# S5 output stage: an even, weighted walk of its list, 8 KB scratch rows, and scan states that reach their operand layout through DRAM

## The chip, the core and the metric

The kernel runs on one core of a Trainium2 chip. The metric is the device time of one execution in microseconds (us), lower is better. Before the change the median of three runs is 1825.99 us (1824.85 to 1827.47).

## What is computed

Two layers over a sequence of 256 frames with 2048 channels: a chunked gated linear attention (GLA), then an S5 state-space layer. Only the second matters here. Cut to its core:

```python
proj = u_in @ w_in                                   # (256, 2048) @ (2048, 8192)
u, z = jnp.split(proj, 2, axis=-1)                   # 4096 channels each, 256 groups of 16
bu = einsum('blgi,gpi->blgp', u, bb)                 # 64 complex states for each group
x = scan over the frames: x[l] = lb * x[l-1] + bu[l]
y = Re(einsum('blgp,gip->blgi', x, c)) + d_skip * u
y = gelu(y)
y = y * sigmoid(y @ w_glu + b_glu) * silu(z)
h = y @ w_out
```

All of it is float32. The large products are made of three products of split operands (a high part and a remainder, `hi` and `lo`).

## The kernel before: its stages and what sets the order

The recurrence is taken in blocks of 8 frames, so a scan runs over 32 blocks (chunks) instead of 256 frames. What a block needs from the state at its start is one product, and what its frames give each other is another, with a Toeplitz operand. The 256 groups are taken 8 at a time, in 32 units `f`.

The stages of the S5 layer, in order of time:

- `su`: the u half of the input projection, in 8 groups of banks. Beside it the block operands are made (`b_pow`, `b_tr`, `s_mm`, `k_out`): the block inputs of the scan go into `sx`, the Toeplitz rows into the DRAM scratch `dk` (512 rows, pitch 1920 floats). A DRAM scratch `rec` (128 rows, 32 units of 384 floats) was filled in the GLA layer with the small tables of each unit.
- `sz`: the z half of the projection, again 8 groups `g` of 8 steps `kp`. A step splits a 512 KB weight tile (`hisz`, cast on ScalarE at L145; `losz`, subtraction on VectorE at L146) and issues 24 matmuls of 128x256. The split tiles have three buffers each, the weight tiles four. A group writes four banks of PSUM, and the pool `mm` has five. So the first quarter of a group's first step finds a free bank, and the second quarter waits until ScalarE has emptied the first bank of the group before (`zs`, SiLU, L1280). Steps are named here by group and step: step 2.0 works with `hisz20`, its banks are `sz20` to `sz23`.
- the S5 output stage: it lies in the shade of the `sz` groups 1 to 7, which are 56 steps. A list of small pieces is walked while the steps go by. In its order it has, for `f` from 0 to 33: up to three of the 30 scan steps of the second half (`scan`, L1183 to L1185), `cside(f)` (loads `cl` for unit f+1 and the Toeplitz tile `mt` for unit f, makes the two 128x1024 operands `wc`), `xstage(f-1)` and `ystage(f-2)`. `pump(Y_RATE)` pops 2.311 pieces at each step, whatever their size.
- `gl`: the GLU product with 4096x4096 weights, which reads the activated outputs `U`.

`xstage(f)` brings the chunk states into the layout of a matmul operand: VectorE turns 32x32 blocks of `sx` (L1237, tile `xT`), TensorE turns two 128x128 tiles of it (L1240, tile `psxs`), ScalarE copies them out of PSUM (L1242, tile `xS`). `ystage(f)` is 24 matmuls of 128x128 with 32 output partitions each: 8 with `mt` (L1252) and 16 with `wc` (L1255), four of them side by side on the array; the hardware has each as two. VectorE then turns the sum (L1258, `yt`), and ScalarE applies the GELU and writes it over `U` (L1259). GELU and SiLU are in different function tables, so a change between L1259 and L1280 loads a table.

`cload` fetches `cl` with three DMAs (L1213 once, L1215 twice, for rows in swapped halves), `mload` fetches `mt` with one DMA of 512 KB (L1229): 16 rows of `dk`, each read eight times, shifted by 512 B. `mt` and `wc` have two buffers, so the load of `mt` for unit f waits for the matmuls of unit f-2.

The order on each engine isn't that of the source. A scheduler of the tile layer places every instruction on its engine, by its own estimate of when its inputs are there; each engine then works strictly in its own order and waits where something isn't there. A DMA that SP or ScalarE issues takes one of eight completion semaphores (`DMAHW0` to `DMAHW7`), which the two queues share, and waits until the transfer that used this semaphore before has landed.

Of the kernel before, what the change touches and what calls it, by code (L numbers as in the profile page):

```python
# [33 lines left out]
def trunk(ctx, tc, x, c, ln_g, ln_b, ada_w, ada_b, gla_w_in, gla_gate_w2, gla_gate_b, gla_norm_g,  # L34
# [393 lines left out]

    vt = cp.tile([P, 104], F32, name="vt")
    gnT, gbT, bgluT, lngT, lnbT = vt[:, 0:32], vt[:, 32:40], vt[:, 40:72], vt[:, 72:88], vt[:, 88:104]  # L430

    def vectors():
        vr = tp.tile([104, P], F32, tag="vr", name="vr", bufs=1)
        rows = [(gla_norm_g[0], 32), (gla_gate_b[0], 8), (s5_b_glu[0], 32), (ln_g[0], 16), (ln_b[0], 16)]
        r0 = 0
        for ap, n in rows:
            dma(vr[r0:r0 + n, :], ap.rearrange("(k p) -> k p", p=P))
            r0 += n
        ps = psx("psv")
        PE.transpose(ps[:, :104], vr, ident[:104, :104])  # L440
        S.copy(vt, ps[:, :104])

    ada0 = ada_now(0, 0, 0, 2)
# [4 lines left out]
    abT = cp.tile([P, 64], F32, name="abT")  # L448
    ps = psx("psv2")
# [21 lines left out]
    dT = cp.tile([16, 256], F32, name="dT")  # L471

    def prep_small():
        dr = rp.tile([P, 2, 16], F32, tag="row", name="dr", bufs=2)
        dma(dr, s5_d[0].rearrange("(h g i) -> g h i", h=2, i=16))
        ps = psx("psd")
        for h in range(2):
            PE.transpose(ps[:16, h * P:(h + 1) * P], dr[:, h, :], ident)
        S.copy(dT, ps[:16, 0:256])
# [121 lines left out]
    def prep_pow(t):  # L601
# [6 lines left out]
        for ri in range(2):  # L608
            for nb in range(2):
# [5 lines left out]
                S.activation(lc[:, :, ri, :, nb * 4:nb * 4 + 4].rearrange("p f g n -> p n f g"), pv, AF.Identity, scale=sgn if ri else 1.0)  # L615
        wdma(rec[:, 16 * t:16 * t + 16, 128:256], lc.rearrange("p f r g n -> p f (r g n)"))

    def to_rows(src, i_of, t, o, nm):
        got = {}

        def step(ib):
# [7 lines left out]
            if ib == 3:  # L629
                av = a.rearrange("p (f g) i -> p f (g i)", f=16)  # L630
                wdma(rec[:, 16 * t:16 * t + 16, o:o + 128], av)

        return [lambda ib=ib: step(ib) for ib in range(4)]

    def prep_b(t):
# [21 lines left out]

        return [load], [comp] + to_rows(lambda: got["b"], lambda s, i: s[:, :, i], t, 256, f"b{t}")

    def prep_c(t):  # L660
# [14 lines left out]

        return [load], [comp] + to_rows(lambda: got["c"], lambda s, i: s[:, i].rearrange("g r p -> g (r p)"), t, 0, f"c{t}")

# [13 lines left out]
    SCAN_RATE = 1.728  # L691
    Y_RATE = 2.311
    qt, kt = qk
# [359 lines left out]
    def bload(f2):  # L1053

        a = tp.tile([P, 2, 384], F32, tag="rb", name=f"rb{f2}", bufs=2)
        dma(a[:, :, 0:256], rec[:, 2 * f2:2 * f2 + 2, 128:384])
        for h in range(2):
            dma(a[64 * h:64 * h + 64, :, 256:384], rec[64 - 64 * h:128 - 64 * h, 2 * f2:2 * f2 + 2, 256:384])
        rb[f2] = a
# [3 lines left out]
    def kload(f2):  # L1063

        a = rc[f2] = tp.tile([P, 2, 144], F32, tag="rc", name=f"rc{f2}", bufs=2)
        dma(a, rec[:, 2 * f2:2 * f2 + 2, 0:144])

# [93 lines left out]
    for p in range(18):  # L1161
# [5 lines left out]
        if p >= 2:  # L1167
            bq.append(lambda p=p: k_out(p - 2))

    bload(0)  # L1170
    b_pace = [0.0]

# [38 lines left out]
    def cload(f):  # L1211
        a = tp.tile([P, 384], F32, tag="cl", name=f"cl{f}", bufs=2)
        dma(a[:, 0:256], rec[:, f, 0:256])  # L1213
        for h in range(2):
            dma(a[64 * h:64 * h + 64, 256:384], rec[64 - 64 * h:128 - 64 * h, f, 0:128])  # L1215
        cl[f] = a

    def cunit(f):
        a = cl[f]
        w = [tp.tile([P, 8, 8, 16], F32, tag=f"wc{i}", name=f"wc{i}{f}", bufs=2) for i in range(2)]  # L1220
        powmul(w[0], w[1], a[:, 0:128], a[:, 256:384], a[:, 128:256])
        wc[f] = w
# [3 lines left out]
    def mload(f):  # L1226
        m = tp.tile([P, 8, 8, 16], F32, tag="mt", name=f"mt{f}", bufs=2)
        src = bass.AP(tensor=kap.tensor, offset=kap.offset + f * 16 * 1920, ap=[[1920, 16], [128, 8], [1, 1024]])
        dma(m.rearrange("p t g i -> p (t g i)"), src)  # L1229
        mt[f] = m  # L1230

    xss = {}

    def xstage(f):
        xt_ = tp.tile([P, 2, 4, 32], F32, tag="xt", name=f"xT{f}", bufs=1)
        n = 2 * (f % 16)
        V.transpose(xt_, sx[:, f // 16, 0:32, :, n:n + 2].rearrange("p c r b -> p b r c"))  # L1237
        px = psx(f"psxs{f}")
        for b in range(2):
            PE.transpose(px[:, b * P:(b + 1) * P], xt_[:, b].rearrange("p r l -> p (r l)"), ident)  # L1240
        xs = tp.tile([P, 2, 128], F32, tag="xs", name=f"xS{f}", bufs=2)
        S.copy(xs, px[:, :T].rearrange("p (b r) -> p b r", b=2))  # L1242
        xss[f] = xs

    def ystage(f):
# [3 lines left out]
        for b in range(2):  # L1249
# [3 lines left out]
            for w in wc[f]:  # L1253
                for q in range(4):
                    PE.matmul(o[32 * q:32 * q + 32], lhsT=xs[:, b, 32 * q:32 * q + 32],  # L1255
                              rhs=w[:, 2 * q + b].rearrange("p n i -> p (n i)"), start=False, stop=(w is wc[f][-1]))
        yt = tp.tile([P, 8, 32], F32, tag="yt", name=f"yt{f}", bufs=2)
        V.transpose(yt, py[:, :T].rearrange("p (b t i) -> p t b i", b=2, t=8))  # L1258
        S.activation(U, yt, AF.Gelu_apprx_tanh)  # L1259

    def cside(f):
# [3 lines left out]
        cunit(f)  # L1265

    zs = []
# [32 lines left out]
    while bg:  # L1300
        pump()

# [149 lines left out]
```

## Time and profile before

| | |
|---|---|
| median of three runs | 1825.99 us |
| profiled execution, its own time | 1828.37 us |
| its span | 1826.6 us |
| TensorE busy in the span | 97% |
| VectorE busy | 77% |
| ScalarE busy | 49% |
| GpSimd busy | 5% |
| S5 output stage (sz groups 1 to 7) | 1050.8 to 1277.6 us, 226.8 us |

Times inside the profile are microseconds from the start of the span. PE is TensorE, PEld its weight loads, DVE VectorE, ACT ScalarE, POOL GpSimd, SP SyncE, which issues nearly all DMAs; a q behind an engine's name is its queue. Matmuls are pipelined, so their busy time is modelled, and the distance from one start to the next tells more than the length of one. A row of a group gives lines, engine, operation, tiles and shapes, the count, then busy time and the mean of one in ns, then idle time of the engine just ahead of them and what ended it. "DMA share" is the mean busy share of the core's 16 DMA engines.

### The profile page before, as it was taken

What the parts mean: (1) busy time and instruction counts of PE and PEld (TensorE: products, weight loads), DVE (VectorE), ACT (ScalarE), POOL (GpSimd) and SP (SyncE); (2) the same over time, 40 slices, a digit from 0 to 9 for tenths busy, and PEclk for the clock granted to TensorE, in tenths of its full rate; (3) what the DMA queues carried; (4) which work ended last, traced back from release to release, by engine and by line L of the source; (5) the groups of instructions that cost most, each with busy time, mean ns of one, the idle gap of its engine ahead of it and who ended that gap; (6) DMA issues with size and microseconds to landing.
All of it is one profiled execution on the core that took longest, in us unless ns stands there. A gap on an engine that the chain in (4) does not pass through costs nothing.

```text
span 1826.6 us, 33659 instructions
## 1 busy us (share of the span) xinstructions
PE 1780.4 (97%) x13491; PEld 1573.1 (86%) x13491; DVE 1411.3 (77%) x1880; ACT 898.9 (49%) x1266; POOL 86.3 (5%) x94
## 2 busy tenths in 40 slices
PE   7999999999999999999999999999999999999997
PEld 5776897899999888799999999989888888888885
DVE  4887757879999988687789789889577775557556
ACT  4433557556556333655555544546545444444332
POOL 0000000000000000002224300000000000000000
PEclk9999999999999999999999999999999999999998
DMA  9996975879889998587666577999788886668553
GB/s 344 387 358 229 296 249 163 277 265 324 288 285 323 331 364 290 175 254 212 193 199 191 171 223 211 242 241 239 227 283 267 275 275 200 189 200 316 195 183 92
DMA packets 246101, 457.86 MB, mean 251 GB/s; under 512 B 19828, under 2 KB 49198, under 8 KB 244662
## 3 DMA queue, kind: packets, MB, share of 16 engines
q1 hardware_dynamic: 239320, 436.02, 74.4%
q0 software_dynamic: 5856, 18.63, 3.1%
q8 instruction: 106, 1.74, 0.4%
q10 hardware_dynamic: 768, 1.05, 0.2%
q14 instruction: 51, 0.42, 0.1%
HBM read 437.01 MB, written 18.61 MB: 249 GB/s over the span
## 4 chain that ended last, share of the span: by engine, by line
PE 83%; DVE 6%; DMA 5%; ACT 3%; issue 3%; SPq 1%; POOL 0%; DVEq 0%; ACTq 0%; POOLq 0%
PE gl L192 13%; PE gl L193 7%; PE op L168 6%; PE op L169 6%; PE op L167 6%; PE v L168 3%; PE z L182 3%; PE z L181 3%; PE z L180 3%; PE v L169 3%; PE v L167 3%; PE sz L180 3%; PE sz L182 2%; PE su L180 2%; PE sz L181 2%
## 5 line engine op out<-in xcount | busy, mean ns | idle before, releaser
L146 DVE TENSOR_TENSOR logl<-wgl,higl 128x1024 fp32r<-128x1024 f32 x128 | 156.7, 1224 | 116.3 <-ACT higl L145 114.6
L145 ACT CAST higl<-wgl 128x1024 fp32r<-128x1024 f32 x128 | 134.3, 1050 | 172.2 <-PE gl L192 165.4
L192 PE MATMUL gl<-yp,higl 128*128 128x512 f32 x512 | 179.9, 396 | 0.1
L192 PE MATMUL gl<-yb,higl 128*128 128x512 f32 x512 | 179.6, 396 | 0.0
L145 ACT CAST hio<-wo 128x1024 fp32r<-128x1024 f32 x95 | 100.2, 1055 | 153.0 <-PE op L169 134.8
L146 DVE TENSOR_TENSOR loo<-wo,hio 128x1024 fp32r<-128x1024 f32 x95 | 116.7, 1230 | 66.4 <-ACT hio L145 64.5
L317 DVE SCALAR_TENSOR_TENSOR acc<-wa,cs,acc 128x512 f32<-128x512 f32 x217 | 163.0, 751 | 2.7
L180 PE MATMUL su<-u1h,hisu 128*128 128x256 f32 x512 | 151.4, 297 | 0.0
L180 PE MATMUL sz<-u1h,hisz 128*128 128x256 f32 x512 | 150.1, 293 | 1.2 <-ACT zs L1280 1.2
L180 PE MATMUL z<-u0h,hiz 128*128 128x256 f32 x512 | 148.7, 290 | 0.0
L182 PE MATMUL su<-u1h,losu 128*128 128x256 f32 x512 | 145.3, 284 | 0.4 <-DVE losu L146 0.4
L182 PE MATMUL sz<-u1h,losz 128*128 128x256 f32 x512 | 144.5, 283 | 1.1 <-DVE losz L146 1.1
L182 PE MATMUL z<-u0h,loz 128*128 128x256 f32 x512 | 144.9, 283 | 0.6 <-DVE loz L146 0.6
L181 PE MATMUL su<-u1l,hisu 128*128 128x256 f32 x512 | 145.1, 284 | 0.0
L181 PE MATMUL z<-u0l,hiz 128*128 128x256 f32 x512 | 144.7, 283 | 0.0
L181 PE MATMUL sz<-u1l,hisz 128*128 128x256 f32 x512 | 144.5, 282 | 0.0
L193 PE MATMUL gl<-yb,logl 128*128 128x256 f32 x512 | 143.0, 279 | 0.0
L193 PE MATMUL gl<-yp,logl 128*128 128x256 f32 x512 | 142.3, 280 | 0.0
L145 ACT CAST hisz<-wsz 128x1024 fp32r<-128x1024 f32 x64 | 67.0, 1050 | 108.4 <-PE sz L181 60.2
L192 PEld LDWEIGHTS gl<-yp,higl 128*128 128x128 f32 x512 | 95.9, 188 | 23.3 <-issue 0.8
L192 PEld LDWEIGHTS gl<-yb,higl 128*128 128x128 f32 x512 | 96.1, 188 | 23.0
L145 ACT CAST hiz<-wz 128x1024 fp32r<-128x1024 f32 x64 | 67.2, 1052 | 89.0 <-PE z L181 79.4
(322 smaller groups left out, 5001.1 us busy)
## 6 DMA issues: line engine op xcount, KB each, us to landing
wgl<-in_s_w_glu SPq DMA_DIRECT2D x128, 512.0 KB, 4.8
wa<-in_ada_w SPq DMA_DIRECT2D x116, 512.0 KB, 5.3
wv<-in_gla_w_in SPq DMA_DIRECT2D x64, 512.0 KB, 6.2
wz<-in_gla_w_in SPq DMA_DIRECT2D x64, 512.0 KB, 5.0
wsu<-in_s_w_in SPq DMA_DIRECT2D x64, 512.0 KB, 4.2
wsz<-in_s_w_in SPq DMA_DIRECT2D x64, 512.0 KB, 5.7
wo<-in_s_w_out SPq DMA_DIRECT2D x64, 512.0 KB, 4.5
a<-in_ada_w SPq DMA_DIRECT2D x31, 1024.0 KB, 10.8
```

The lines of the kernel that those rows point to most:

```text
L145: S.copy(hi, w)
L146: last_lo[0] = V.tensor_tensor(lo, w, hi.bitcast(F32), op=ALU.subtract).ins
L167: PE.matmul(banks[tt], lhsT=uh, rhs=hi[:, kk, :], start=(k == first), stop=False)
L168: PE.matmul(banks[tt], lhsT=uh, rhs=lo[:, kk, :], start=False, stop=False)
L169: last_mm[0] = PE.matmul(banks[tt], lhsT=ul, rhs=hi[:, kk, :], start=False, stop=(k == last)).ins
L180: PE.matmul(o, lhsT=wh, rhs=u.hi(k), start=(k == first), stop=False)
L181: PE.matmul(o, lhsT=wh, rhs=u.lo(k), start=False, stop=False)
L182: last_mm[0] = PE.matmul(o, lhsT=wl, rhs=u.hi(k), start=False, stop=(k == last)).ins
L192: PE.matmul(banks[f], lhsT=hi[:, kk, fs], rhs=u.both(k), start=(k == 0), stop=False)
L193: PE.matmul(banks[f][:, :T], lhsT=lo[:, kk, fs], rhs=u.hi(k), start=False, stop=(k == last))
L317: V.scalar_tensor_tensor(acc[0], w[:, kk, :], cs[:, k:k + 1], acc[0], op0=ALU.mult, op1=ALU.add)
```

## The change

Four edits go together.

1. **The list.** `bg` and `Y_RATE` give way to a list `yq` of pieces with weights: 1.0 for a scan step, 2.5 for `cside`, 0.5 for `xwrite`, 0.0 for `xread`, 2.0 for `ystage`. The weights add up to 190, and each of the 56 steps is owed 190/56 of them; a piece is issued as soon as its weight is covered. There are two scan steps for each unit instead of three.
2. **Scratch rows.** A unit of `rec` takes 512 floats instead of 384 (a row of `rec` is 64 KB instead of 48), and a row of `dk` 2048 instead of 1920 (8 KB). The extra place in `rec` holds the tables with swapped halves, written by four more DMAs in the GLA layer, so that `cl` comes in one DMA with pieces of 1.5 KB.
3. **Scan states through DRAM.** `xstage` gives way to `xwrite` and `xread`. `xwrite(f)` copies the states of unit f on ScalarE into a dense tile `xT` (L1244, three buffers) and writes it to the DRAM scratch `dx` by a DMA on ScalarE's queue (L1245, 128 rows of 1 KB). `xread(f)` reads it back in operand layout on GpSimd's queue (L1249, tile `xS`, three buffers, pieces of 256 B). The two transposes of TensorE, the one of VectorE and the copy out of PSUM are gone. The partitions of `cl`, `wc` and `xS` are in another order (chunk, then quarter) to fit.
4. **Room.** `vt`, `abT` and `dT` leave the constant pool (`dT` goes through a DRAM scratch and is loaded again), and `yt` has one buffer instead of two.

```diff
-    rec = dp.tile([P, 32, 384], F32, name="rec")
-    dk = dp.tile([512, 1920], F32, name="dk")
+    rec = dp.tile([P, 32, 512], F32, name="rec")
+    dk = dp.tile([512, 2048], F32, name="dk")
+    dx = dp.tile([32, P, 256], F32, name="dx")
...
+                if o == 128:
+                    for h in range(2):
+                        wdma(rec[64 * h:64 * h + 64, 16 * t:16 * t + 16, 0:128], av[64 - 64 * h:128 - 64 * h])
...
     def cload(f):
         a = tp.tile([P, 384], F32, tag="cl", name=f"cl{f}", bufs=2)
-        dma(a[:, 0:256], rec[:, f, 0:256])
-        for h in range(2):
-            dma(a[64 * h:64 * h + 64, 256:384], rec[64 - 64 * h:128 - 64 * h, f, 0:128])
+        dma(a, rec[:, f, 0:384].rearrange("(r l) x -> l r x", r=4))
...
-    def xstage(f):
-        xt_ = tp.tile([P, 2, 4, 32], F32, tag="xt", name=f"xT{f}", bufs=1)
+    def xwrite(f):
+        xt_ = tp.tile([P, 4, 2, 32], F32, tag="xt", name=f"xT{f}", bufs=3)
         n = 2 * (f % 16)
-        V.transpose(xt_, sx[:, f // 16, 0:32, :, n:n + 2].rearrange("p c r b -> p b r c"))
-        px = psx(f"psxs{f}")
-        for b in range(2):
-            PE.transpose(px[:, b * P:(b + 1) * P], xt_[:, b].rearrange("p r l -> p (r l)"), ident)
-        xs = tp.tile([P, 2, 128], F32, tag="xs", name=f"xS{f}", bufs=2)
-        S.copy(xs, px[:, :T].rearrange("p (b r) -> p b r", b=2))
-        xss[f] = xs
+        S.copy(xt_, sx[:, f // 16, 0:32, :, n:n + 2].rearrange("p c r b -> p r b c"))
+        S.dma_start(dx[f], xt_.rearrange("p r b c -> p (r b c)"))
+
+    def xread(f):
+        xs = xss[f] = tp.tile([P, 4, 2, 32], F32, tag="xs", name=f"xS{f}", bufs=3)
+        wdma(xs.rearrange("p q b c -> p q (b c)"), dx[f].rearrange("(q l) (r x) -> (l r) q x", q=4, r=4))
...
-            pump(SCAN_RATE if g == 0 else Y_RATE)
+            if g == 0:
+                pump(SCAN_RATE)
+            else:
+                owed += yrate
+                while yq and owed >= yq[0][0]:
+                    owed -= yq[0][0]
+                    yq.pop(0)[1]()
...
+            yq.append((0.5, lambda: xwrite(0)))
             for f in range(34):
-                for _ in range(3):
-                    if sc1:
-                        bg.append(sc1.pop(0))
+                yq.extend((1.0, sc1.pop(0)) for _ in range(2) if sc1)
                 if f < 32:
-                    bg.append(lambda f=f: cside(f))
-                if 1 <= f < 33:
-                    bg.append(lambda f=f: xstage(f - 1))
+                    yq.append((2.5, lambda f=f: cside(f)))
+                    if f < 31:
+                        yq.append((0.5, lambda f=f: xwrite(f + 1)))
+                    yq.append((0.0, lambda f=f: xread(f)))
                 if f >= 2:
-                    bg.append(lambda f=f: ystage(f - 2))
+                    yq.append((2.0, lambda f=f: ystage(f - 2)))
+            yrate = sum(w_ for w_, _ in yq) / 56
```

How the change stands on two engines is shown by the built programs. First ScalarE at the start of the stage, before: from the cast for step 1.3 on, the casts of the weights follow each other, with a copy of turned states (`xS`, unit number behind it) between.

```order
L145 CAST hisz13_11540<-wsz13_11538 128x1024
L145 CAST hisz14_11591<-wsz14_11589 128x1024
L145 CAST hisz15_11629<-wsz15_11627 128x1024
L145 CAST hisz16_11676<-wsz16_11674 128x1024
L1242 COPY xS0_11583<-psxs0_11580 128x256
L145 CAST hisz17_11742<-wsz17_11740 128x1024
L145 CAST hisz20_11794<-wsz20_11792 128x1024
L1242 COPY xS1_11672<-psxs1_11669 128x256
```

ScalarE at the same place after the change, with the semaphores that an instruction waits for (`DMAHW` ones are transfers):

```order
L145 CAST hisz13_11555<-wsz13_11553 128x1024 [waits DMAHW2_49,PE_49]
L1244 COPY xT0_11453<-sx_7551 128x256 [waits DMASW4_49,DMAHW7_49,DMASW3_49,Pool_49]
L1244 COPY xT1_11502<-sx_7551 128x256
L1245 DMA dx_205<-xT0_11453 128x256 [waits Activation_49]
L1245 DMA dx_205<-xT1_11502 128x256 [waits Activation_49]
L1244 COPY xT2_11583<-sx_7551 128x256
L145 CAST hisz14_11598<-wsz14_11596 128x1024 [waits DMAHW3_49,PE_49]
L1245 DMA dx_205<-xT2_11583 128x256 [waits DMAHW4_49,Activation_49]
L1244 COPY xT3_11634<-sx_7551 128x256 [waits DMAHW0_49]
L1244 COPY xT4_11743<-sx_7551 128x256 [waits DMAHW2_49]
L1245 DMA dx_205<-xT3_11634 128x256 [waits DMAHW6_49,Activation_49]
L1245 DMA dx_205<-xT4_11743 128x256 [waits DMAHW7_49,Activation_49]
```

The scheduler has moved the writes of the first 16 units, whose states are all there when the stage begins, ahead of their place in the list: all 16 copies and DMAs stand between the casts for steps 1.3 and 2.1, two to four copies between two casts. The writes of units 16 to 31 stand in the same way between the casts for steps 4.3 and 5.1. In each of these stretches a copy waits for the write three units earlier, because `xT` has three buffers. In the first, write 5 waits for the semaphore of the load `mt0`. The SiLU copies of group 1 (`zs` from `sz10` to `sz13`) stand behind the cast for step 2.1 and one GELU, in both programs.

The other place is TensorE at the end of the stage. Before, from the last matmuls of unit 30 on (`x4` is four of them):

```order
L1255 MATMUL psy30_14585<-wc030_14408,xS30_14518 32x128 x4
L1255 MATMUL psy30_14585<-wc130_14409,xS30_14518 32x128 x4
L180 MATMUL sz70_14218<-u1h1_7422,hisz76_14615 128x256
L181 MATMUL sz70_14218<-u1l1_7424,hisz76_14615 128x256
L182 MATMUL sz70_14218<-u1h1_7422,losz76_14616 128x256
```

Here unit 30 comes ahead of step 7.6, unit 31 ahead of step 7.7. After:

```order
L1261 MATMUL psy30_14528<-wc030_14365,xS30_14372 32x128 x4
L1261 MATMUL psy30_14528<-wc130_14366,xS30_14372 32x128 x4
L1258 MATMUL psy31_14560<-mt31_14462,U3_7557 32x128 x4
L1261 MATMUL psy31_14560<-wc031_14464,xS31_14468 32x128 x4
L1261 MATMUL psy31_14560<-wc131_14465,xS31_14468 32x128 x4
L1258 MATMUL psy31_14560<-mt31_14462,U3_7557 32x128 x4
L1261 MATMUL psy31_14560<-wc031_14464,xS31_14468 32x128 x4
L1261 MATMUL psy31_14560<-wc131_14465,xS31_14468 32x128 x4
L192 MATMUL gl00_14604<-yp0_14600,higl00_14610 128x512
```

Unit 29 now stands ahead of step 7.7, and units 30 and 31 follow each other behind it, ahead of the first matmul of the GLU product. In the middle of the stage a unit comes every second step up to unit 13 and two units every three steps from there on; before, they came at two in three to five steps while the scan steps lasted, and then mostly one at every step with a gap in each fourth or so.

More of the change, by code (lines that the diff above doesn't have):

```diff
@@ L441, in vectors @@
         S.copy(vt, ps[:, :104])
+        S.copy(bgluT, bglu_)
     ada0 = ada_now(0, 0, 0, 2)
@@ L478, in prep_small @@
             PE.transpose(ps[:16, h * P:(h + 1) * P], dr[:, h, :], ident)
-        S.copy(dT, ps[:16, 0:256])
+        dt_ = rp.tile([16, 256], F32, tag="row", name="dt_", bufs=2)
+        S.copy(dt_, ps[:16, 0:256])
+        wdma(dd, dt_)
         zt = rp.tile([P, 448], F32, tag="row", name="zt", bufs=2)
@@ L615, in prep_pow @@
                 S.activation(lc[:, :, ri, :, nb * 4:nb * 4 + 4].rearrange("p f g n -> p n f g"), pv, AF.Identity, scale=sgn if ri else 1.0)
-        wdma(rec[:, 16 * t:16 * t + 16, 128:256], lc.rearrange("p f r g n -> p f (r g n)"))
+        wdma(rec[:, 16 * t:16 * t + 16, 256:384], lc.rearrange("p f r g n -> p f (r g n)"))
     def to_rows(src, i_of, t, o, nm):
@@ L656, in comp @@
             got["b"] = bb.rearrange("g r p i -> g (r p) i")
-        return [load], [comp] + to_rows(lambda: got["b"], lambda s, i: s[:, :, i], t, 256, f"b{t}")
+        return [load], [comp] + to_rows(lambda: got["b"], lambda s, i: s[:, :, i], t, 384, f"b{t}")
     def prep_c(t):
@@ L674, in comp @@
             got["c"] = cc
-        return [load], [comp] + to_rows(lambda: got["c"], lambda s, i: s[:, i].rearrange("g r p -> g (r p)"), t, 0, f"c{t}")
+        return [load], [comp] + to_rows(lambda: got["c"], lambda s, i: s[:, i].rearrange("g r p -> g (r p)"), t, 128, f"c{t}")
     (lb0, cb0), (lc0, cc0), (lb1, cb1), (lc1, cc1) = prep_b(0), prep_c(0), prep_b(1), prep_c(1)
@@ L1055, in bload @@
         a = tp.tile([P, 2, 384], F32, tag="rb", name=f"rb{f2}", bufs=2)
-        dma(a[:, :, 0:256], rec[:, 2 * f2:2 * f2 + 2, 128:384])
+        dma(a[:, :, 0:256], rec[:, 2 * f2:2 * f2 + 2, 256:512])
         for h in range(2):
-            dma(a[64 * h:64 * h + 64, :, 256:384], rec[64 - 64 * h:128 - 64 * h, 2 * f2:2 * f2 + 2, 256:384])
+            dma(a[64 * h:64 * h + 64, :, 256:384], rec[64 - 64 * h:128 - 64 * h, 2 * f2:2 * f2 + 2, 384:512])
         rb[f2] = a
@@ L1065, in kload @@
         a = rc[f2] = tp.tile([P, 2, 144], F32, tag="rc", name=f"rc{f2}", bufs=2)
-        dma(a, rec[:, 2 * f2:2 * f2 + 2, 0:144])
+        dma(a, rec[:, 2 * f2:2 * f2 + 2, 128:272])
     def powmul(o, t, a0, a1, l):
@@ L1168, in trunk @@
             bq.append(lambda p=p: k_out(p - 2))
+    dT = tp.tile([16, 256], F32, tag="dT", name="dT", bufs=1)
+    dma(dT, dd)
     bload(0)
```

25 lines of the change are left out of this document (13 added, 12 removed).

## Prediction

> **What bounds the kernel now.** I read the engine line of the page first, then the busy times of the output stage in two parts, then the waits of TensorE there.
>
> ```profile
> PE 1780.4 (97%) x13491; PEld 1573.1 (86%) x13491; DVE 1411.3 (77%) x1880; ACT 898.9 (49%) x1266; POOL 86.3 (5%) x94
> ```
>
> ```profile
> core 0: us, PE busy (x) PEld busy (x) DVE busy (x) ACT busy (x) POOL busy (x), PEclk, DMA share, GB/s
> 1050.80:1277.60 226.80, 221.62 (x2946) 209.28 (x2945) 204.51 (x290) 115.45 (x178) 1.95 (x3) 1.00 0.89 232
> 1050.80:1150.00 99.20, 96.92 (x1152) 92.93 (x1150) 92.37 (x161) 45.70 (x68) 1.95 (x3) 1.00 0.80 222
> 1150.00:1277.60 127.60, 124.69 (x1802) 116.35 (x1795) 112.14 (x130) 69.75 (x111) 0.00 (x0) 1.00 0.96 239
> ```
>
> ```profile
> PE psy L1252 <- DMA mt<-dk: 1.8, 3, 1.0
> PE sz L180 <- ACT zs L1280: 1.2, 2, 1.0
> PE psy L1252 <- ACT U L1259: 1.1, 1, 1.1
> PE sz L182 <- DVE losz L146: 1.1, 1, 1.1
> ```
>
> TensorE is the bound: it idles only 226.8 - 221.6 = 5.2 us of the stage, and the four waits add up to just that. So the stage ends when TensorE's work and its waits are done, and a gain is work taken from TensorE or one of these waits. The second thing to see is the last row: the DMA engines are at 0.96 in the dense part, so they are nearly as full as TensorE.
>
> What a step and a unit cost TensorE is read from its timeline, by distances between starts.
>
> ```profile
> 1148.26 0.28 PE L182 MATMUL sz<-u1h,losz 128*128 128x256 f32 x1
> 1148.38 0.38 PE L1240 MATMUL psxs<-ident,xT 128*128 128x128 f32 x2
> ...
> 1150.14 0.38 PE L180 MATMUL sz<-u1h,hisz 128*128 128x256 f32 x1
> 1150.36 0.28 PE L181 MATMUL sz<-u1l,hisz 128*128 128x256 f32 x1
> ...
> 1152.75 0.28 PE L180 MATMUL sz<-u1h,hisz 128*128 128x256 f32 x1
> 1152.87 0.28 PE L181 MATMUL sz<-u1l,hisz 128*128 128x256 f32 x1
> 1152.99 0.28 PE L182 MATMUL sz<-u1h,losz 128*128 128x256 f32 x1
> 1153.11 0.38 PE L1240 MATMUL psxs<-ident,xT 128*128 128x128 f32 x2
> 1153.25 0.36 PE L180 MATMUL sz<-u1h,hisz 128*128 128x256 f32 x1
> 1153.45 0.28 PE L181 MATMUL sz<-u1l,hisz 128*128 128x256 f32 x1
> ```
>
> A matmul of `sz` starts 0.12 us after the last, so a step of 24 is 2.88. From 1152.87 to 1153.45 stand three such distances, 0.36, and 0.58 have gone by: a pair of transposes costs 0.22. From 1148.26 to 1150.36 stand two distances (0.24), one pair (0.22) and one unit: 2.10 - 0.46 = 1.64, say 1.6. The sum closes: 56 x 2.88 + 32 x 1.6 + 32 x 0.22 + 5.2 = 161.3 + 51.2 + 7.0 + 5.2 = 224.7 of 226.8.
>
> **The change, part by part.**
>
> *Transposes.* 32 pairs leave TensorE: 32 x 0.22 = **-7.0**. They stood on the bounding engine, so all of it counts, if nothing new is waited for.
>
> *The list.* Between the `mt` loads stands the distance of units f-2 and f. In the dense part units came at nearly every step, now two come in three steps, so the two buffers cover the landing and I take the waits for `mt` away: **-1.8** (bounds -1.8 and 0). The one wait for `losz` came behind a transpose `xT` on VectorE that is gone now.
>
> ```profile
> L1237 DVE STREAM_TRANSPOSE xT<-sx 128x256 f32<-128x256 f32 x32 | 20.2, 631 | 0.2
> ```
>
> That takes about 0.6 of the 1.1: **-0.6**. VectorE loses 20.2 us in all, but it isn't last elsewhere. The waits for `zs` (1.2) and `U` (1.1) I leave.
>
> *The writes of units 0 to 15 on ScalarE.* Here the change adds a wait. The casts, the table loads and `zs` of group 1 are queued behind 16 copies and DMA issues; each copy waits until the write three units earlier has landed, and write 5 for `mt0`. No row of before has this write or this copy, so both are bounded.
>
> ```profile
> wsz<-in_s_w_in SPq DMA_DIRECT2D x49, 512.0 KB, 6.0
> mt<-dk SPq DMA_DIRECT2D x32, 512.0 KB, 7.8
> cl<-rec SPq DMA_DIRECT2D x32, 128.0 KB, 3.1
> cl<-rec SPq DMA_DIRECT2D x64, 32.0 KB, 6.5
> dk<-ks POOLq DMA_DIRECT2D x2, 64.0 KB, 2.2
> ```
>
> ```profile
> L1259 ACT ACTIVATE U<-yt 128x256 f32<-128x256 f32 x32 | 13.3, 415 | 9.4 <-DVE yt L1258 9.2
> L1259 ACT ACT_TABLE_LOAD x9 | 11.5, 1283 | 2.6 <-DVE yt L1258 2.4
> L1280 ACT ACTIVATE zs<-sz 128x256 f32<-128x256 f32 x28 | 10.1, 389 | 4.4 <-PE sz L182 4.1
> ...
> L925 ACT ACTIVATE z<-z 128x256 f32<-128x256 f32 x32 | 18.4, 684 | 0.2
> ```
>
> ```profile
> L1408 ACTq DMA_DIRECT2D out<-big x16: 321/427/443, 1810.2 to 1823.2; - x16
> ```
>
> The landing L lies between 2.2 (64 KB, a write) and 3.1 (128 KB, the same size, but a read); I take 2.6, the middle. The copy lies between 0.41 (`U`, dense) and 0.68 (`z`, strided); I take 0.41, its shape. The issue is 0.43. In the order, writes 5, 8, 11 and 14 form a chain of three links, each one landing, one copy and one issue of the neighbour: L + 0.84 = 3.4. Write 5 can't go before `mt0` is there.
>
> ```profile
> 1053.73 1.05 ACT L145 CAST hisz<-wsz 128x1024 fp32r<-128x1024 f32 x1 [1.97 <-PE sz L181]
> 1056.62 1.05 ACT L145 CAST hisz<-wsz 128x1024 fp32r<-128x1024 f32 x1 [1.83 <-PE sz L181]
> ```
>
> ```profile
> 1055.00 0.34 SPq L1213 DMA_DIRECT2D cl<-rec  x1
> ...
> 1056.55 0.58 SPq L1213 DMA_DIRECT2D cl<-rec  x1
> ```
>
> The first cast is that for step 1.3, which starts when step 1.0 ends. `mt0` is issued behind two loads `cl`, at 1055.0 + 0.34 + 0.58 or about 1056.0, so it lands about 1063.8. Three links later it is 1074.1. Behind write 14 come copy and write 15 (0.41 + 0.43), the cast for 2.1 (1.05), a table load, a GELU and a table load (1.28 + 0.41 + 1.28), and the `zs` (0.39): 5.7 with the issue of write 14. The casts for 1.5 to 2.0 that don't fall into a wait I put at 1.5, an estimate from walking the queue by hand with these rows. So `zs` of `sz10` is there at 1074.1 + 5.7 + 1.5 = 1081.3. TensorE needs it after a quarter of step 2.0: 1053.7 + 7 x 2.88 + two units of 1.6 + the 0.5 left of the `losz` wait + 0.72 = 1078.3. The stall is **+3.0**; with L = 2.2 three links give back 1.2 (+1.8), with L = 3.1 they add 1.5 (+4.5), and a copy of 0.68 adds at most 1.4.
>
> [...]
>
> *The writes of units 16 to 31* stand the same way from the cast for 4.3 to that for 5.1, where two or three units more stand in TensorE's own way, so the same chain comes nearer to its time: **+1.0**, between 0 (L = 2.2) and 2.5 (L = 3.1).
>
> *The end.* Now units 30 and 31 both follow step 7.7, and the load of `mt31` waits for unit 29, ahead of that step. Issue and landing against the cover:
>
> ```profile
> 1265.14 0.53 SPq L1229 DMA_DIRECT2D mt<-dk  x1
> ```
>
> 0.53 + 7.8 = 8.3, against step 7.7 and unit 30, 2.88 + 1.6 = 4.5: a wait of **+3.8**. With a landing of 6.0, as `wsz` of the same size has, it is 2.0; never below 0.
>
> *What I cost at nothing.* `xread` goes on GpSimd's queue, which is idle (1.95 us busy in the stage); the read is wanted two units later, some 10 us, against a landing between 2.2 and 6.5 (pieces of 512 B; here 256 B). Without that cover each unit would wait 2 us or more. SP's loads share eight semaphores with the writes and can wait up to L for one; four weight tiles cover it. One DMA for `cl` saves two issues on SP. The four DMAs into `rec` in the GLA layer, the reload of `dT` and the single `yt` stand far from any of the four waits; 0, at most one landing of 2.2 each.
>
> *Sum.* -7.0 - 1.8 - 0.6 + 3.0 + 1.0 + 3.8 = -1.6. The profiled span is 1826.6, its own time 1828.37, which stand 0.6 and 2.4 above the median of 1825.99; the sum holds against its own stage, so I apply it to the median: 1824.4.
>
> **The rivals.**
>
> *The new waits hardly show.* For it: L may be 2.2, and at the end the queues thin out, so `mt31` may land sooner. Then -9.4 + 1.8 + 0 + 0 to 1 is about -7.5: **1818**. Against it: all 32 loads of `mt` took 7.1 us or more.
>
> ```profile
> DMA to landing us min/median/max: 7.1/7.8/7.8
> ```
>
> *The DMA engines become the bound* (slower). The stage moved this much:
>
> ```profile
> DMA packets 29442, 52.53 MB, mean 232 GB/s; under 512 B 2992, under 2 KB 11184, under 8 KB 29411
> ```
>
> At a share of 0.89 that is 202 us of full engines, 3.84 us a MB. `dx` adds 32 x 2 x 131 KB = 8.4 MB, at that price 32 us: 234, which is 7 more than the stage has. The time is then about **1833**. It decides from the point at which the MB costs over 226.8 / 60.9 = 3.7 us. Against it: where weights alone stream, the page's third slice moves 387 GB/s at a share over 0.9, 2.4 us a MB, and then 222 us suffice; and the even walk moves loads from the part with 0.96 to the part with 0.80.
>
> ```profile
> GB/s 344 387 358 229 296 249 163 277 265 324 288 285 323 331 364 290 175 254 212 193 199 191 171 223 211 242 241 239 227 283 267 275 275 200 189 200 316 195 183 92
> DMA  9996975879889998587666577999788886668553
> ```
>
> *The new pitch slows the loads.* Rows of `x` lie 64 KB apart, as those of `rec` do now, and land late:
>
> ```profile
> big<-in_x SPq DMA_DIRECT2D x8, 256.0 KB, 11.6
> ```
>
> Were that the pitch's doing, 192 KB of `cl` would take three quarters, 8.7. A unit has 226.8 / 32 = 7.1 us and `cl` is fetched one unit ahead, so with the issue (0.34) each unit runs 1.9 late, 62 us in all: about **1888**. Against it: the rows of `wsz` are 32 KB apart and 512 KB land in 6.0, and the load of `x` stands at the start of the kernel among full queues. [...]
>
> *The freed time is not used*: the stage keeps its pace because VectorE or a transfer sets it, **1826**. VectorE was busy 204.5 of 226.8 and loses 20, which speaks against it.
>
> **How the numbers follow.** A difference under 0.2%, 3.7 us, is about what a measurement of this kernel can't tell from none, so "same" is 1822.3 to 1829.6. The forecast, 1824.4 with its own spread of 1821 to 1829 from the bounds of L, copy and end, gets 0.44 (0.10 of it faster, 0.34 same). Hidden waits, 1818: 0.25, faster. Full DMA engines, 1833: 0.22, slower. Pitch: 0.04, slower. Unused time: 0.05, same. Together faster 0.35, same 0.39, slower 0.26. The range goes from the floor in which no wait of the stage is left (161.3 + 51.2 + 2.1 = 214.6, -12.2, 1814) to a little over the case of full DMA engines: 1814 to 1836.
>
> **What the profile of the changed kernel would show.** Right: no `psxs`, TensorE's work in the stage down by 7; a wait of `sz` for `zs` of about 3 us in step 2.0 and about 1 in step 5.0; a wait of `psy` for `mt` of some 4 us at the end, and none in the middle; `dx` writes landing in 2.2 to 3.1. The hidden case would show the landings near 2.2 and none of the three waits over 1 us. Full DMA engines would show a share near 1.0 in the whole stage, `wsz` and `mt` landing later than 6.0 and 7.8, and waits for `hisz` behind DMA. The pitch would show in `cl` landing over 7 us. I am wrong in the mechanism if TensorE waits for `xS`, or if the stage is longer while the DMA share is not higher than 0.9.

## The result and the profile after

| | before | after |
|---|---|---|
| median | 1826.73 us (1824.85 to 1828.86, 4 runs) | 1855.03 us (1853.89 to 1857.74, 4 runs) |
| ratio, 95% interval | | 1.0151 (1.0135 to 1.0167) |
| profiled span | 1826.6 us | 1853.3 us |
| start of step 1.0 | 1050.8 | 1059.6 |
| start of step 1.0 to the first matmul of `gl` | 226.9 us | 244.2 us |
| from there to the end of the span | 548.9 us | 549.4 us |

The change is slower by 28 us, outside the range of 1814 to 1836. The last three rows are read from TensorE's timeline: 8.9 us of the profile's 26.7 were lost ahead of the stage, 17.3 in it, 0.5 behind it. The lines of after that answer to those of before, first the engines on the page:

```profile
PE 1785.8 (96%) x13427; PEld 1577.2 (85%) x13427; DVE 1395.2 (75%) x1848; ACT 903.8 (49%) x1264; POOL 114.9 (6%) x131
```

The busy times of the stage and its two parts, with the granted clock, the DMA share and the rate as the last three columns:

```profile
core 0: us, PE busy (x) PEld busy (x) DVE busy (x) ACT busy (x) POOL busy (x), PEclk, DMA share, GB/s
1059.70:1303.90 244.20, 220.30 (x2882) 208.06 (x2881) 193.77 (x263) 124.79 (x181) 25.96 (x35) 0.96 0.93 253
1059.70:1160.00 100.30, 87.17 (x1008) 83.34 (x1008) 79.61 (x134) 47.27 (x66) 11.00 (x15) 0.93 0.85 236
1160.00:1303.90 143.90, 133.13 (x1876) 124.72 (x1874) 114.16 (x130) 77.52 (x116) 14.96 (x20) 0.98 0.98 265
```

TensorE has 64 matmuls fewer, but idles 23.9 us where it idled 5.2, and its clock is 0.96 where it was 1.00. What it waited for there:

```profile
PE sz L180 <- ACT zs L1293: 11.3, 2, 10.4
PE psy L1258 <- DMA mt<-dk: 4.7, 3, 2.6
PE sz L180 <- ACT hisz L145: 4.4, 1, 4.4
PE sz L182 <- DVE losz L146: 3.4, 3, 1.9
```

All three waits for `mt` stand behind 1290 us, at the end of the stage; in the middle there is none. The two waits for ScalarE are the news. ScalarE's own waits in the stage, and the group of the new copies, say why:

```profile
ACT xT L1244 <- DMA dx<-xT: 28.2, 15, 5.7
```

```profile
L1244 ACT COPY xT<-sx 128x256 f32<-128x256 f32 x32 | 20.3, 650 | 29.8 <-DMA dx<-xT 28.2 <-ACT xT L1244 1.3 <-DMA dk<-ks 0.3
```

And the transfers of the stage, with KB each and the median us to landing. Such a median is taken over the transfers whose landing the trace tells: here 6 of the 32 `mt`, 5 of the 32 `cl`, 9 of the 32 writes `dx` and all 32 reads `xS`.

```profile
DMA packets 30986, 61.90 MB, mean 253 GB/s; under 512 B 3022, under 2 KB 11214, under 8 KB 30957
...
wsz<-in_s_w_in SPq DMA_DIRECT2D x49, 512.0 KB, 6.1
mt<-dk SPq DMA_DIRECT2D x32, 512.0 KB, 7.5
cl<-rec SPq DMA_DIRECT2D x32, 192.0 KB, 7.4
dx<-xT ACTq DMA_DIRECT2D x32, 128.0 KB, 2.9
xS<-dx POOLq DMA_DIRECT2D x32, 128.0 KB, 7.1
```

The first burst on ScalarE, from the issue of writes 3 and 4 on (copies L1244, issues L1245, waits in brackets; copies and writes are counted from 0):

```profile
1068.23 0.96 ACTq L1245 DMA_DIRECT2D dx<-xT  x2
...
1076.58 0.66 ACT L1244 COPY xT<-sx 128x256 f32<-128x256 f32 x1 [3.20 <-DMA dx<-xT]
1076.64 1.03 ACTq L1245 DMA_DIRECT2D dx<-xT  x2
...
1081.71 0.88 ACTq L1245 DMA_DIRECT2D dx<-xT  x2
...
1086.14 0.66 ACT L1244 COPY xT<-sx 128x256 f32<-128x256 f32 x1 [1.86 <-DMA dx<-xT]
1086.15 1.01 ACTq L1245 DMA_DIRECT2D dx<-xT  x2
...
1092.04 0.63 ACT L1244 COPY xT<-sx 128x256 f32<-128x256 f32 x1 [3.12 <-DMA dx<-xT]
...
1093.73 0.33 ACTq L1245 DMA_DIRECT2D dx<-xT  x1
1095.21 0.62 ACT L1244 COPY xT<-sx 128x256 f32<-128x256 f32 x1 [1.51 <-DMA dx<-xT]
...
1100.37 1.21 ACT L1293 ACTIVATE zs<-sz 128x256 f32<-128x256 f32 x4
```

Write 3 is issued at 1068.23, writes 5 and 6 at 1076.64, 8 and 9 at 1081.71, 10 and 11 at 1086.15, 14 at 1093.73. Write 3 had landed at 1076.6, when copy 6 could start; write 8 at 1086.1, when copy 11 could; write 10 at 1092.0, when copy 13 could. These are landings of 8.3, 4.4 and 5.9, read from what they release; the median of 2.9 above stands on 9 other landings. So `zs` of group 1 comes at 1100.37, 40.7 us into the stage, and TensorE stands:

```profile
1089.66 0.36 PE L182 MATMUL sz<-u1h,losz 128*128 128x256 f32 x1
...
1100.80 0.58 PE L180 MATMUL sz<-u1h,hisz 128*128 128x256 f32 x1 [10.43 <-ACT zs L1293]
1101.18 0.42 PE L181 MATMUL sz<-u1l,hisz 128*128 128x256 f32 x1
1101.40 0.41 PE L182 MATMUL sz<-u1h,losz 128*128 128x256 f32 x1
```

### The profile page after: what moved, and what is told of

It is laid out like the page before. It is cut to its first block, busy times and chain, and to the rows that moved or that the text cites. A ratio compares the mean times of both kernels' runs of the same rounds, so it can differ in the third digit from the quotient of the medians.

```text
span 1853.3 us, 33501 instructions
## 1 busy us (share of the span) xinstructions
PE 1785.8 (96%) x13427; PEld 1577.2 (85%) x13427; DVE 1395.2 (75%) x1848; ACT 903.8 (49%) x1264; POOL 114.9 (6%) x131
## 5 line engine op out<-in xcount | busy, mean ns | idle before, releaser
L180 PEld LDWEIGHTS sz<-u1h,hisz 128*128 128x128 f32 x512 | 100.0, 195 | 23.0 <-ACT zs L1293 11.9
L146 DVE TENSOR_TENSOR losz<-wsz,hisz 128x1024 fp32r<-128x1024 f32 x64 | 78.3, 1226 | 51.3 <-ACT hisz L145 47.8
```

The lines of the kernel that those rows point to most:

```text
L146: last_lo[0] = V.tensor_tensor(lo, w, hi.bitcast(F32), op=ALU.subtract).ins
L180: PE.matmul(o, lhsT=wh, rhs=u.hi(k), start=(k == first), stop=False)
```

## The experiments

The theory after the result: ScalarE's queue of copies makes the long waits. Its rival: the DMA engines are full (share 0.98 in the second part), and what TensorE waits for is only where this shows. For the 8.9 us ahead of the stage: the four writes of the swapped tables against the other moves.

| kernel | median us | ratio to before, 95% interval | profiled run | start | stage |
|---|---|---|---|---|---|
| no_swapped_place | 1853.63 | 1.0152 (1.0137 to 1.0167) | 1851.29 | 1051.2 | 248.9 |
| copy_on_gpsimd | 1853.48 | 1.0149 (1.0134 to 1.0165) | 1851.57 | 1057.3 | 243.8 |
| transposes_back | 1833.61 | 1.0040 (1.0025 to 1.0055) | 1835.47 | 1057.6 | 227.1 |
| list_alone | 1827.23 | 1.0000 (0.9988 to 1.0011) | 1831.13 | 1054.6 | 225.1 |
| half_mt_gpsimd | 1837.58 | 1.0050 (1.0033 to 1.0067) | 1831.07 | 1055.5 | 226.7 |
| no_read_of_dx | 1847.91 | 1.0112 (1.0096 to 1.0128) | 1846.48 | 1055.1 | 241.2 |
| list_end_spread | 1825.73 | 0.9993 (0.9984 to 1.0003) | 1822.65 | 1050.1 | 222.6 |
| changed_end_spread | 1858.76 | 1.0165 (1.0145 to 1.0184) | 1863.47 | 1056.9 | 255.4 |
| transposes_no_swapped | 1827.83 | 1.0010 (0.9998 to 1.0022) | 1829.60 | 1054.4 | 224.1 |
| half_mt | 1839.23 | 1.0071 (1.0058 to 1.0084) | 1838.59 | 1057.9 | 231.8 |
| half_mt_7_buffers | 1824.13 | 0.9985 (0.9976 to 0.9994) | 1821.35 | 1056.0 | 216.2 |
| gpsimd_no_swapped | 1846.35 | 1.0099 (1.0077 to 1.0120) | 1849.94 | 1051.5 | 247.1 |

The runs of before beside them had medians of 1826.8 to 1827.0. Start and stage are from one profile each, read as in the first table. The profiled run can stand up to 6.5 us from the median of its kernel (half_mt_gpsimd), so a difference of medians is the measure, and the stages tell where it lies.

**no_swapped_place.**

```diff
-                if o == 128:
-                    for h in range(2):
-                        wdma(rec[64 * h:64 * h + 64, 16 * t:16 * t + 16, 0:128], av[64 - 64 * h:128 - 64 * h])
...
-        dma(a, rec[:, f, 0:384].rearrange("(r l) x -> l r x", r=4))
+        dma(a, rec[:, f, 128:512].rearrange("(r l) x -> l r x", r=4))
```

> The four writes of the swapped tables into rec (512 KB each) are left out, and the load of cl reads the other three tables of the same size in their place, so its values are wrong and its transfers keep their shape. Theory: these writes delay the weight tiles wz at the end of the value and gate projections, and make the 9 us that the stage begins late (1059.7 against 1050.8 us). Then the stage begins at 1051 to 1053 and the time is about 1847. Rival: the late start comes from the other moves ahead of the stage (tiles taken out of the constant pool, the reload of dT). Then the start stays over 1057 and the time over 1852.

The start is back at 1051.2, as the theory has it, but the time is only 1.4 us below the changed kernel, where 8 were expected: the stage took 248.9, with 9.2 us of waits for `mt` against 4.7.

**copy_on_gpsimd.**

```diff
-        S.copy(xt_, sx[:, f // 16, 0:32, :, n:n + 2].rearrange("p c r b -> p r b c"))
-        S.dma_start(dx[f], xt_.rearrange("p r b c -> p (r b c)"))
+        nc.gpsimd.tensor_copy(xt_, sx[:, f // 16, 0:32, :, n:n + 2].rearrange("p c r b -> p r b c"))
+        wdma(dx[f], xt_.rearrange("p r b c -> p (r b c)"))
```

> The copy into xT and the write to dx go to GpSimd and its queue; the rest is the changed kernel. Theory: the stage is long because ScalarE stands in copies that wait for landings, with zs and the casts behind them (waits of TensorE of 11.3 us for zs and 4.4 for hisz, and a lower granted clock behind them). Then both waits fall under 2 us, the clock stays near 1.00 in the stage, and the time is about 1836. Rival: the DMA engines are full (share 0.93 in the stage, 0.98 in its second part), and the time only moves to waits for wsz, mt or xS: over 1848.

The waits of TensorE there:

```profile
PE psy L1258 <- DMA mt<-dk: 10.1, 11, 2.0
PE psy L1261 <- DMA xS<-dx: 7.4, 1, 7.4
PE sz L182 <- DVE losz L146: 3.3, 2, 3.0
PE sz L180 <- ACT zs L1293: 1.7, 3, 0.9
```

ScalarE is out of the way, as expected, and nothing is gained: the stage is 243.8 and the time goes to eleven waits for `mt` and one for `xS`, whose read stood behind copies on GpSimd's queue. The theory of ScalarE alone, by which the time would be about 1836, fell here.

**transposes_back.** `xstage` and the layout of `cl`, `xS` and `yt` as before the change, the rest as after; the list then reads

```diff
-                    if f < 31:
-                        yq.append((0.5, lambda f=f: xwrite(f + 1)))
-                    yq.append((0.0, lambda f=f: xread(f)))
+                if 1 <= f < 33:
+                    yq.append((0.5, lambda f=f: xstage(f - 1)))
```

> The third edit alone is undone: the states go through VectorE and TensorE again, with the weighted list, the new pitch and the four writes into rec kept. Theory: the way through DRAM costs its own gain of 7 us and 17 more. Then the stage is at most 226 us, the start stays 9 late, and the time is 1833 to 1837. Rival: list or pitch hold the stage up: over 1845.

1833.61, inside the expected range: the third edit costs 21.4 us beside the other three, 17.1 of them in the stage by the profiles. The stage is 1 us longer than the 226 that were expected at most.

**list_alone** (the kernel before with the list, the same pieces as in transposes_back).

> The kernel before with the first edit alone: the weighted list, with the transposes as a piece of weight 0.5. Theory of the prediction: the waits for mt in the middle (1.8 us) go and one of about 3 to 4 us at the end comes: 1826 to 1829, no difference that can be measured. Rival: the even pace is worth more than the end costs: under 1822.

No difference, as expected: the stage is 225.1, with a wait of 2.0 for `mt` at its end in place of those in the middle. Its start at 1054.6, with nothing changed ahead of it, shows how far single profiles scatter there: 4 us.

**half_mt_gpsimd** (copy_on_gpsimd, and in `mload` and `ystage`):

```diff
-        m = tp.tile([P, 8, 8, 16], F32, tag="mt", name=f"mt{f}", bufs=2)
+        m = tp.tile([P, 8, 4, 16], F32, tag="mt", name=f"mt{f}", bufs=2)
...
-        src = bass.AP(tensor=kap.tensor, offset=kap.offset + f * 16 * 2048, ap=[[2048, 16], [128, 8], [1, 1024]])
+        src = bass.AP(tensor=kap.tensor, offset=kap.offset + f * 16 * 2048, ap=[[2048, 16], [128, 8], [1, 512]])
...
-                PE.matmul(o[32 * q:32 * q + 32], lhsT=U[:, 2 * q + b], rhs=mt[f][:, :, 2 * q + b, :], start=True, stop=False)
+                PE.matmul(o[32 * q:32 * q + 32], lhsT=U[:, 2 * q + b], rhs=mt[f][:, :, (2 * q + b) % 4, :], start=True, stop=False)
```

> As copy_on_gpsimd, but a load of mt brings only half of its columns (256 KB in pieces of 2 KB) and the products read that half twice, so the values of y are wrong; every matmul stays. It takes 8.4 MB off the DMA engines, as much as dx adds. Theory (formed on the first four runs): the DMA engines are full, and with the waits of ScalarE out of the way they alone hold the stage at 244 us. Then the waits for mt and xS (10.1 and 7.4 us) fall under 3 together, the stage to 216 to 222 us and the time to 1826 to 1832. Rival: single late transfers or GpSimd's own order hold it, not the load: over 1845.

```profile
PE sz L182 <- DVE losz L146: 3.8, 2, 3.1
PE psy L1261 <- DMA xS<-dx: 3.8, 1, 3.8
PE sz L180 <- ACT zs L1293: 2.8, 3, 1.8
```

The same matmuls, the same DMAs in number, 8.4 MB less: the waits for `mt` are gone, the stage is 17.1 shorter and the median 15.9 lower. It misses the expected range by 6, with a profile of the fastest of its five runs, and a read of `xS` late on GpSimd's queue stays (3.8). So with the ring of three buffers (copy, write, landing, next copy) on GpSimd, the load of the engines holds the stage up: their share falls from 0.92 in copy_on_gpsimd to 0.78.

**no_read_of_dx**.

```diff
-        wdma(xs.rearrange("p q b c -> p q (b c)"), dx[f].rearrange("(q l) (r x) -> (l r) q x", q=4, r=4))
+        nc.gpsimd.memset(xs, 0.0)
```

> The changed kernel without the read of dx: xS is set to zero by GpSimd, so the carried states are missing from y; the copies and writes on ScalarE stay. It takes 4.2 MB off the DMA engines. Theory: ScalarE's queue makes the wait for zs in step 2.0 by its own three buffers and the landing of a write, whatever the engines do else: that wait stays above 6 us, and the waits for mt and the second burst shrink, time 1840 to 1848. Rival (full engines make the landings late, and these the bursts): wait for zs under 3, time under 1838.

```profile
PE sz L180 <- ACT zs L1293: 11.9, 2, 9.8
...
PE psy L1258 <- DMA mt<-dk: 1.2, 2, 0.7
```

The time is in the expected range. The waits for `mt` shrink with the load, but step 2.0 still waits 9.8: the first burst doesn't hang on the reads.

**list_end_spread and changed_end_spread.** The same edit in list_alone and in the changed kernel:

```diff
-                    yq.append((2.0, lambda f=f: ystage(f - 2)))
-            yrate = sum(w_ for w_, _ in yq) / 56
+                    yq.append((2.0 if f < 32 else 3.45, lambda f=f: ystage(f - 2)))
+            yrate = sum(w_ for w_, _ in yq) / 54.5
```

> The kernel before with the weighted list, as list_alone, and the end of the list paced apart: the weights are walked in 54.5 steps and the last two ystage weigh 3.45, so that units 29, 30 and 31 stand ahead of steps 7.5, 7.6 and 7.7. Theory: the wait at the end, 2.3 to 4 us, shrinks to about 1, and with it 2 us against list_alone: 1823 to 1825. Rival: the waits for mt only move ahead by a few steps: 1827.

The waits for `mt` are gone from its profile and the stage is 222.6, the shortest with transposes; the median is 1.5 below list_alone and 0.7 above the expected range, and against before the interval reaches from 0.9984 to 1.0003, so it can't be told from no change.

> The changed kernel with the same end of the list as list_end_spread. Theory of the prediction: the wait at the end (4.1 us behind step 7.7 and 1.3 ahead of it) goes, 1850 to 1852. Rival (full DMA engines): the time only moves to waits for mt ahead of the end, 1855.

```profile
PE psy L1258 <- DMA mt<-dk: 10.8, 4, 3.6
PE sz L180 <- ACT zs L1293: 7.5, 2, 4.2
PE sz L180 <- ACT hisz L145: 5.6, 2, 3.0
PE sz L182 <- DVE losz L146: 4.6, 5, 1.9
```

Slower by another 3.7: the wait moved to four places ahead of the end and grew. `mt` lands in 9.9 instead of 7.5, `wsz` in 9.0 instead of 6.1. I read it as a quicker walk that asks the full engines (a share of 0.92 in this stage) for the same bytes sooner; no run tests this by itself. Here the theory of the prediction failed and the rival was nearer, on its far side.

**transposes_no_swapped.**

```diff
-                if o == 128:
-                    for h in range(2):
-                        wdma(rec[64 * h:64 * h + 64, 16 * t:16 * t + 16, 0:128], av[64 - 64 * h:128 - 64 * h])
...
-        dma(a, rec[:, f, 0:384])
+        dma(a[:, 128:384], rec[:, f, 128:384])
+        for h in range(2):
+            dma(a[64 * h:64 * h + 64, 0:128], rec[64 - 64 * h:128 - 64 * h, f, 128:256])
```

> As transposes_back, but without the four writes of 512 KB into rec; cl comes in three transfers as before, with the new pitch. Theory: those writes are what makes transposes_back (1833.6) slower than list_alone (1827.2), so this is 1826 to 1828. Rival (the pitch or the moves of tiles): 1831 or more.

1827.83, as expected: without the four writes, and with `cl` in three transfers again, the time is 5.8 us below transposes_back. List, pitch and moves of tiles together are not to be told from nothing.

**half_mt and half_mt_7_buffers.** The load of half_mt_gpsimd in the changed kernel, with ScalarE's copies and three buffers; then with

```diff
-        xt_ = tp.tile([P, 4, 2, 32], F32, tag="xt", name=f"xT{f}", bufs=3)
+        xt_ = tp.tile([P, 4, 2, 32], F32, tag="xt", name=f"xT{f}", bufs=7)
```

> The changed kernel, its copies on ScalarE, with the half load of mt of half_mt_gpsimd (values of y wrong, same matmuls). Theory of two limits: with the DMA engines relieved the first burst still stands in ScalarE's queue with three buffers, so TensorE waits over 6 us for zs in step 2.0, and the time is 1840 to 1846, above the 1837.6 of half_mt_gpsimd. Rival (late landings make the burst): wait for zs under 3, time at most 1837.

> As half_mt, with seven buffers for xT in the room that the half mt leaves. Theory: the wait for the write three units earlier makes the burst; with seven buffers the copies wait for almost nothing, the wait for zs falls under 4 us (16 copies and issues still take 16 us of ScalarE) and the time is 4 to 7 below half_mt. Rival: the semaphores shared with late loads make the burst; then within 2 us of half_mt.

TensorE's waits in half_mt:

```profile
PE sz L180 <- ACT zs L1293: 11.1, 2, 9.2
PE sz L182 <- DVE losz L146: 2.5, 2, 1.7
PE sz L180 <- ACT hisz L145: 1.2, 1, 1.2
```

and in half_mt_7_buffers:

```profile
PE sz L182 <- DVE losz L146: 1.8, 1, 1.8
PE sz L180 <- ACT zs L1293: 0.7, 2, 0.4
```

In half_mt TensorE waits 9.2 us for `zs` in step 2.0, as expected (over 6), and the time is 0.8 under the expected range. Four more buffers take 15.6 us from the stage and 15.1 from the median, more than twice what I expected. They don't do it by quicker landings: the median of those that the trace tells is 4.3 us with seven buffers and 2.7 with three, while the copies wait 21.7 us for earlier writes with three and not at all with seven. So there are two limits, each shown by taking it away alone: the ring of three buffers (231.8 against 216.2 with the engines relieved) and the load of the engines (243.8 against 226.7 with the ring on GpSimd). Seven buffers with the whole load of `mt` were not run, so the load without any ring isn't measured. half_mt_7_buffers reads half of an operand, so its 1824.13 is no kernel to use. It shows what the way through DRAM is worth without both limits: a stage of 216.2, near the floor of 214.6 that the prediction worked out.

**gpsimd_no_swapped** (copy_on_gpsimd with the edit of no_swapped_place).

> As copy_on_gpsimd, without the four writes into rec and with the load of cl reading three other tables in the same shape (values wrong). Theory: the stage begins 5 to 8 us earlier and stays as long, 1846 to 1848. Rival (as no_swapped_place hinted): the full engines take the earlier start back, 1851 to 1854.

1846.35 is in the expected range and 7.1 below copy_on_gpsimd, though its four runs spread from 1836.9 to 1849.9: the writes cost here about what they cost with transposes. Why no_swapped_place gave back most of this stays open.

## Why the prediction was wrong

**What failed, in short.** Two terms of the sum. The landing of a write was put too low, so the first burst, +3.0, became a wait of 10.4 us. And the four DMAs into `rec` were put at nothing and cost 5.8 to 7.1. One loss had no term at all: behind the waits of 10.4 and 4.4 us TensorE's granted clock was 0.50. In the stage the account closes: the waits grow from 5.2 to 23.9, +18.7 where +5.4 was forecast; the transposes take 7.0 away, as forecast; and TensorE's busy time falls by 1.3 instead of 7.0, so 5.7 go to slower work (last section). That is 18.7 - 7.0 + 5.7 = 17.4.

**The transposes, -7.0:** right in kind. The stage of half_mt_7_buffers, 216.2 with 2.5 us of waits, leaves no room for 7 us of other work beside 161.3 and 51.2.

**The waits for `mt` in the middle, -1.8:** right. The changed kernel has none there, and its 4.7 us all belong to the end; list_alone keeps 0.3 in the middle, list_end_spread has none at all. The reason given against sooner landings, that all 32 loads of `mt` took 7.1 us or more, stands on less than it says: the trace of before tells 3 of these 32 landings.

**The first burst, +3.0:** the right place, the right queue, and forecast at a third of its size. The copy takes 0.65, not 0.41, so the upper bound of 0.68 was the nearer row: I went by the shape of the tile, while the input of the copy is strided, which I take for the reason; no run tests it. The landing was 4.4 to 8.3 for the writes on which the burst hung (3, 5, 8 and 10), not 2.6, and outside my bounds of 2.2 and 3.1. The bounds were badly drawn: 2.2 is the median of two `dk` writes, where all 32 of before have 2.1 to 4.8, and 3.1 stands on the 4 of 32 `cl` loads whose landing the trace tells, which have 2.3 to 7.8. Write 5 left 17.0 us into the stage (1076.6 against 1059.6) instead of 13.0, and not for `mt0`: copy 6, ahead of it on the queue, had to wait for write 3, which landed 8.3 after its issue. The three links to write 14 (1093.7) took 17.1 instead of 10.3. These 4.0 and 6.8 are, to 0.6 us, the 10.2 by which `zs` came later than worked out (40.7 against 30.5 us after the start of the stage). TensorE itself came 3.1 later than worked out (30.6 against 27.5), 2.6 of it in waits for `losz` in steps 1.4 and 1.7, whose casts stand in the same queue; so the wait grew by 7.4 only. That the ring is enough for such a wait is shown by half_mt (9.2) and half_mt_7_buffers (0.4).

The spread over the 9 writes whose landing the trace tells, to which the 8.3 of write 3 doesn't belong:

```profile
DMA to landing us min/median/max: 1.7/2.9/6.4
```

**The second burst, +1.0:** 4.4 for `hisz` in step 4.7 and 0.8 for `zs` in step 5.0, by the same links.

**The end, +3.8:** right in size, in part by luck. From the start of step 7.7 (1294.0) to the first matmul of `gl` (1303.8) are 9.8 us, and 2.88 + 2 x 1.6 = 6.1 of them are work: 3.7 more. But they are two waits, 1.1 for the `mt` of unit 30 and 2.6 for that of unit 31, where one of 3.8 was forecast, and unit 29 ahead of the step waits another 1.0.

**The rest at nothing:** here a step failed outright. "The four DMAs into `rec` in the GLA layer ... stand far from any of the four waits" counted four small writes; they are 512 KB each, and they don't have to meet a wait of the stage, only one of their own place. Before, ScalarE waited for `wz` there:

```profile
ACT hiz L145 <- DMA wz<-in_gla_w_in: 4.7, 1, 4.7
```

After, on ScalarE and then on TensorE, which waits for copies that are queued behind this cast; and the writes in that stretch:

```profile
ACT hiz L145 <- DMA wz<-in_gla_w_in: 8.4, 1, 8.4
```

```profile
PE psst L856 <- ACT sts L860: 2.8, 1, 2.8
```

```profile
rec<-rowsc POOLq DMA_DIRECT2D x2, 512.0 KB, 10.1
```

All eight profiles with the writes show this wait of 2.5 to 2.8 for `sts`, the six without them none. Their starts are 1055.1 to 1059.6 with, 1050.1 to 1054.6 without; the medians give 5.8 and 7.1. ScalarE's wait for `wz` is 3.7 us longer here than before; where the writes cost the rest was not traced.

**The rivals.** The one of full DMA engines (slower, 1833, at 0.22) had the right sign and one of the two limits, and its sum for the stage's engines was close: 234 us of full engines was worked out, and 0.93 x 244.2 = 227 measured. What failed is the step from there to the time: I let the stage be as long as the engines' sum, with one limit at a time. But a landing already took 8.3 us in the first part, at a share of 0.85, and landings stand in the ring on ScalarE. Of this rival's signs only a part came: a share of 0.98, but in the second part alone; `wsz` landed in 6.1 and `mt` in 7.5, where before had 6.0 and 7.8; and no cast waited for `wsz`. The price set against it, 387 GB/s, is that of the second slice of the profile's page; the third has 358. The two signs that I had named for a wrong mechanism, a wait for `xS` and a share not above 0.9, didn't come. The rival of the pitch is refuted: its sign did show, `cl` landing in 7.4, but transposes_back loads the same rows and lands them in 4.1, half_mt in 3.5 (each a median of 4 or 5 landings), and transposes_no_swapped has the new pitch at a ratio of 1.0010. So it was the load (a DMA share of 0.93 in the changed kernel's stage, of 0.87 and 0.76 in those two), and the rounding of the rows to 8 and 64 KB did no harm that these runs can measure.

## What to carry to other kernels

Taking work off the bounding engine by sending it through memory paid here only where the DMA engines had room in the same stretch (a stage of 216.2 us at a share of 0.81 in half_mt_7_buffers, of 244.2 at 0.93 in the changed kernel): look at their share there first, and take the landing of a new transfer from rows of loaded stretches, with their maximum, not from the nearest size. Such a median can stand on a few landings (9 of 32 for `dx`); the wait that a landing ends tells it too. A ring of buffers on an engine that also feeds the bound puts a landing into every turn (4.4 to 8.3 us here); work out the turn with the slow landing, and count whose instructions stand behind it. Price each added transfer by its bytes in the place where it runs, also far from the change: four of 512 KB cost 5.8 to 7.1 us here.

## What the runs showed of the hardware that was not expected

TensorE paid twice for its two longest waits. After the 10.4 us of the first burst its granted clock is 0.50, and a matmul of `sz` starts every 0.21 us instead of 0.12 (1101.18 and 1101.40 above). The stretches ahead of that wait, in its second half and twice behind it, with PEclk as the third value from the end:

```profile
1085.00:1089.50 4.50, 4.46 (x71) 4.12 (x72) 2.63 (x6) 2.30 (x3) 0.00 (x0) 1.00 0.88 244
```

```profile
1094.00:1100.00 6.00, 0.00 (x0) 0.00 (x0) 2.50 (x6) 4.29 (x5) 0.00 (x0) 0.50 0.35 108
```

```profile
1100.00:1104.90 4.90, 4.10 (x19) 4.10 (x20) 4.87 (x8) 3.99 (x8) 0.00 (x0) 0.50 0.82 226
```

```profile
1104.90:1110.00 5.10, 5.10 (x74) 4.76 (x73) 3.06 (x8) 2.19 (x3) 0.00 (x0) 0.84 0.60 175
```

Some 25 matmuls ran at that pace, and 20 more behind the wait of 4.4 us for `hisz` in step 4.7, where the clock is 0.50 again from 1192.65 to 1198.08: by estimate 45 x 0.09 = 4 us, the larger part of the 5.7 above. Products `psy` in this stretch are slower too: the half unit that starts at 1197.65 takes 1.16 us to the start of the next, the one at 1203.72, at a clock of 1.00, 0.68. half_mt_7_buffers, whose longest wait is 1.8 us, shows the same work at the full clock, with 213.7 us busy where the changed kernel has 220.3:

```profile
1056.30:1272.50 216.20, 213.73 (x2881) 202.84 (x2880) 191.47 (x261) 123.35 (x178) 25.95 (x35) 1.00 0.81 245
```

The clock came back 5.7 us after work began at 1100.8: it is 0.50 in the quarter of a microsecond up to 1106.50 and 0.98 in the one behind it.
